# Merge-gate projections by Strassen's seven block products, with stored activation sums, in a hybrid attention block

## The chip, the core and the metric

The kernel runs on one core of a Trainium2 chip. The metric is the device time of one execution in microseconds, as the median of several runs. The engines are called by the names of the profile: PE (TensorE, the matrix engine; PEld is its weight load), DVE (VectorE), ACT (ScalarE), POOL (GpSimd) and SP (SyncE, which issues most DMAs here).

## The reference

One decoder layer over 512 tokens of width 1024, in float32:

```python
h = rms_norm(x, norm_g)                       # (512, 1024)
proj = h @ w_in                               # (1024, 6152)
fq, fk, fv, fz, mq, mk, mv, mz, ga, gb, fl = split_cols(proj, IN_SPLITS)
# 8 x 512 columns, then 1024 (ga), 1024 (gb), 8 (fl)
q, k = rms_norm(heads(fq), fox_q_g), rms_norm(heads(fk), fox_k_g)
log_f = log_sigmoid(fl + b_f)
y_fox = fox_attention(q, k, heads(fv), log_f) * silu(fz)      # 8 heads of 64
q, k = rope(rms_norm(heads(mq), moba_q_g)), rope(rms_norm(heads(mk), moba_k_g))
y_moba = moba_attention(q, k, heads(mv)) * silu(mz)           # 8 heads of 64
merged = (sigmoid(ga + b_gate[0]) * (y_fox @ w_fox)
          + sigmoid(gb + b_gate[1]) * (y_moba @ w_moba))
out = x + merged @ w_out
```

The two merge gates, `ga` and `gb`, are products of the normalised activations (512 x 1024) with 1024 columns of weights each. They are what the change is about. With two key blocks and a top-k of three, MoBA keeps every earlier block, so the kernel computes it as causal attention.

## The kernel before

Every matrix product is made of three matmuls on operands that are split in a high part and a remainder (`wh`/`wl` for weights, `Gh`/`Gl` for activations, `pth`/`ptl` for attention weights): high x high, high x remainder, remainder x high.

**Activations.** `load_g` reads the transposed x in 8 tiles of 128 x 512 (128 features, 512 tokens), multiplies them by `norm_g` and splits them into `Gh` (ACT) and `Gl` (DVE). They aren't divided by the root mean square. `x_stats` finds the factor `r` of each token later, from the untransposed x, and `x_bc` makes `rbc`, `r` spread over all partitions, by four transposes into the bank `p_rbc` and a copy on ACT. Each result is multiplied by `r` or `rbc` when it leaves PSUM: z units by DVE (`V.tensor_tensor(out=z, in0=p, in1=rbc, ...)`, tiles `zs_…`), then a sigmoid on ACT and a product on POOL; values by `evac_v`; queries and keys by the head norm `norm_qk`, whose small power `ff` and product `qn` are on POOL. POOL also applies the rotation in `do_rope`.

**Weights.** They come in chunks of 256 columns, in two halves of 4 x 128 rows each (512 KB). `load_half` issues a load on SP's queue into one of two buffers `wr` and calls `split`: ACT writes `wh` (128x1024), and the remainder `wl` is written in two pieces of 128x512, one on DVE and one on POOL (for `fka` and `fza` both on DVE). `load_branch` does the same for `w_fox` and `w_moba`, 512 columns at a time, and `load_out` for `w_out`. The chunks are named by projection and half: `fqa` is the first half of fq, `mzb` the second of mz; `ga0` to `ga3` and `gb0` to `gb3` are the gates, `wf0`, `wf1`, `wm0`, `wm1`, `wo0` to `wo3` the rest.

**Gates.** A gate unit makes 128 columns for all 512 tokens (`tr_mm`, lines 287 to 295): 8 row tiles x 3 matmuls of 512 columns, into a bank `pj`. `unit_ga` multiplies by `rbc`, applies the sigmoid and multiplies by the FoX branch `FS` (made by `unit_f`); `unit_gb` keeps the sigmoid for `unit_m`, which adds both branches and splits the merged rows into `mgh`, `mgl` for the output projection (`first_o`, `unit_o`).

**Order.** Each engine works off its own queue in order. The order of the program below is written by hand; when the kernel is built, a scheduler's timeline may still move single instructions within it. The program starts with `fqa` and `fka` over all tokens at once (`first_qk`), then x_stats, the z gates, the first values, and the forget gates (`forget`: a chain of small 128x32 DVE instructions `fg`, a cumulative sum by matmuls into `p_c`, and a table `LR` by transposes into `p_LR`). Then there are four attention groups of four heads. Each has steps `Tr` (transposes into `p_qT`, `p_kT`, splits, and copies of `KH` between partitions by DMA), `Aa` (scores and softmax; `lg`), `Bb` (transposes of the weights, their split, value matmuls into `pv`, and the pair `ypair`), `Yp` (product with the z gate and its split). `inter` mixes these steps with projection units:

```python
seq(["fza", "fzb", "fva"])
forget()
inter(attn_group("f", "a", ...), filler(["fqb", "fkb", "fvb"]))
inter(attn_group("f", "b", ...), filler(["mqa", "mka", "mva"]))
moba_begin()
seq(["mza", "mzb"])
inter(attn_group("m", "a", ...), filler(["mqb", "mkb", "mvb"]))
inter(attn_group("m", "b", ...), filler(["wf0", "wf1", "ga0"]))
seq(["ga1", "ga2", "ga3", "gb0", "gb1", "wm0", "gb2", "gb3", "wm1"])
first_o()
seq(["wo1", "wo2", "wo3"])
```

`filler` issues the loads and splits of the next chunk after the first unit of the present one.

## Time and profile before

| | before |
|---|---|
| runs, us | 442.98 (median), 442.8, 444.35 |
| span of the profiled execution, us | 440.8 |
| that execution's own time | the page gives none beside the span; the runs lie 2.0 to 3.6 us above the span |
| busy: PE / DVE / ACT / POOL, us | 433.9 / 277.9 / 231.1 / 178.1 |
| matmuls | 2804 |
| data moved by DMA | 45.85 MB, 104 GB/s on average |
| granted clock of TensorE | 9 tenths or more in all slices |

The profile is one execution on the chip, in microseconds from the start of its span. An engine's busy time is what its own instructions take; register and semaphore instructions and the issuing of DMAs are not in it. A row of the timeline gives start, duration, engine, line, operation, output and inputs, shape, and in brackets how long the engine had been idle before it and what it waited for. Grouped rows give the count, the total, and the mean in nanoseconds; rows by tile give minimum, median and maximum in nanoseconds and the stretch in which they lie. The page's part 2 divides the span into 40 slices of 11.0 us with the busy share in tenths.

### The profile page before, as it was taken

The page shows a single profiled execution, that of the slowest core. Times are in us where ns is not written, and L with a number is a line of the kernel's source. Part 1 is how long each engine was busy: PE and PEld are TensorE (multiplying, and loading weights), DVE is VectorE, ACT ScalarE, POOL GpSimd, SP SyncE. Part 2 cuts the span into 40 slices and gives each one's busy share as a digit, 9 for nine tenths or more (in the row PEclk, how much of TensorE's full clock was granted, in tenths as well). Part 3 has the DMA queues.
Part 4 walks back from the last instruction along what each step waited for, and adds up shares of the span by engine and source line. Part 5 has one row for each costly group of instructions (what it writes and reads, how often), then busy time and mean ns, then how long its engine had stood idle before and what let it go on. Part 6 is the DMA issues. An engine that isn't in the chain of part 4 may idle for free.

```text
span 440.8 us, 7535 instructions
## 1 busy us (share of the span) xinstructions
PE 433.9 (98%) x2804; PEld 394.0 (89%) x2804; DVE 277.9 (63%) x606; ACT 231.1 (52%) x439; POOL 178.1 (40%) x159
## 2 busy tenths in 40 slices
PE   7999999999999999999999999999999999999996
PEld 6998899999999998889999888888888888889996
DVE  4649626999789896248977868786442482373311
ACT  5866237867766754357866677564333333331200
POOL 6059624327347472555575222052333333322400
PEclk9999999999999999999999999999999999999999
DMA  8942225312243022231220422122222223335511
GB/s 256 366 151 100 95 97 148 95 55 99 65 105 121 3 94 97 95 120 25 96 97 1 145 81 75 36 97 90 96 101 86 91 72 114 116 119 160 189 62 48
DMA packets 18933, 45.85 MB, mean 104 GB/s; under 512 B 2576, under 2 KB 6800, under 8 KB 18896
## 3 DMA queue, kind: packets, MB, share of 16 engines
q1 hardware_dynamic: 16160, 43.13, 30.5%
q10 hardware_dynamic: 2736, 2.23, 1.5%
q8 instruction: 22, 0.36, 0.3%
q14 instruction: 15, 0.12, 0.1%
HBM read 39.98 MB, written 2.10 MB: 95 GB/s over the span
## 4 chain that ended last, share of the span: by engine, by line
PE 93%; DMA 2%; DVE 2%; ACT 1%; issue 0%; SPq 0%; ACTq 0%
PE pga L295 3%; PE pgb L295 3%; PE pga L294 3%; PE pga L293 3%; PE pgb L294 3%; PE pgb L293 3%; PE po L608 3%; PE po L609 3%; PE po L610 3%; PE lg L428 2%; PE pv L458 2%; PE lg L429 2%; PE pv L457 2%; PE pf L508 2%; PE pm L510 2%; PE pf L510 2%
## 5 line engine op out<-in xcount | busy, mean ns | idle before, releaser
L433 ACT ACTIVATE p<-p,negm 128x128 f32<-128x128 f32 (+1 forms) x64 | 35.7, 560 | 27.1 <-DVE negm L431 26.7
L222 POOL TENSOR_TENSOR ff<-ss,mh 128x8 f32<-128x8 f32 x16 | 27.9, 1750 | 34.3 <-DVE ss L220 31.1
L431 DVE CUSTOM_DVE_ANT_0 p<-lg,mask 128x128 f32<-128x128 f32 (+1 forms) x64 | 30.7, 485 | 11.3 <-PE lg L429 10.6
L436 DVE TENSOR_SCALAR p<-p,rinv 128x128 f32<-128x128 f32 (+1 forms) x64 | 31.3, 497 | 1.2
L102 POOL TENSOR_TENSOR wl_wo<-wr_o,wh_wo 128x512 fp32r<-128x512 f32 x8 | 14.1, 1758 | 32.8 <-ACT wh_wo L99 32.8
L608 PE MATMUL po<-wh_wo,mgh 128*128 128x256 f32 x96 | 27.1, 282 | 0.0
L610 PE MATMUL po<-wh_wo,mgl 128*128 128x256 f32 x96 | 26.9, 281 | 0.0
L609 PE MATMUL po<-wl_wo,mgh 128*128 128x256 f32 x96 | 26.9, 281 | 0.0
L102 POOL TENSOR_TENSOR wl_gb<-wr_gb,wh_gb 128x512 fp32r<-128x512 f32 x8 | 14.3, 1787 | 31.0 <-ACT wh_gb L99 31.0
L293 PE MATMUL pga<-Gh,wh_ga 128*128 128x512 f32 x64 | 25.6, 400 | 0.0
L102 POOL TENSOR_TENSOR wl_ga<-wr_ga,wh_ga 128x512 fp32r<-128x512 f32 x8 | 12.1, 1516 | 33.2 <-ACT wh_ga L99 28.6
L294 PE MATMUL pga<-Gl,wh_ga 128*128 128x512 f32 x64 | 25.5, 399 | 0.0
L295 PE MATMUL pga<-Gh,wl_ga 128*128 128x512 f32 x64 | 25.4, 397 | 0.0
L295 PE MATMUL pgb<-Gh,wl_gb 128*128 128x512 f32 x64 | 25.3, 395 | 0.0
L293 PE MATMUL pgb<-Gh,wh_gb 128*128 128x512 f32 x64 | 25.2, 393 | 0.0
L294 PE MATMUL pgb<-Gl,wh_gb 128*128 128x512 f32 x64 | 25.2, 393 | 0.0
L428 PE MATMUL lg<-KH,QS 128*128 128x128 f32 (+1 forms) x64 | 20.7, 329 | 0.5 <-DMA KH<-KH 0.4
L618 DVE TENSOR_TENSOR ot<-po,xr 128x256 f32<-128x256 f32 x16 | 6.6, 424 | 22.2 <-PE po L610 17.4
L99 ACT ACTIVATE wh_wo<-wr_o 128x1024 fp32r<-128x1024 f32 x8 | 8.5, 1061 | 21.6 <-DMA out_dram<-ot 8.0
L609 PEld LDWEIGHTS po<-wl_wo,mgh 128*128 128x128 f32 x96 | 18.1, 189 | 0.0
L610 PEld LDWEIGHTS po<-wh_wo,mgl 128*128 128x128 f32 x96 | 18.1, 189 | 0.0
L608 PEld LDWEIGHTS po<-wh_wo,mgh 128*128 128x128 f32 x96 | 18.1, 189 | 0.0
(389 smaller groups left out, 1628.5 us busy)
## 6 DMA issues: line engine op xcount, KB each, us to landing
wr_ga<-in_w_in_dram SPq DMA_DIRECT2D x8, 512.0 KB
wr_gb<-in_w_in_dram SPq DMA_DIRECT2D x8, 512.0 KB
wr_o<-in_w_out_dram SPq DMA_DIRECT2D x8, 512.0 KB
xt<-in_xT_dram SPq DMA_DIRECT2D x8, 256.0 KB
x<-in_x_dram SPq DMA_DIRECT2D x8, 256.0 KB
KH<-KH SPq DMA_DIRECT2D x16, 128.0 KB
wr_wf<-in_w_fox_dram SPq DMA_DIRECT2D x4, 512.0 KB
wr_wm<-in_w_moba_dram SPq DMA_DIRECT2D x4, 512.0 KB
```

The lines of the kernel that those rows point to most:

```text
L102: eng.tensor_tensor(out=lo[:, q, 0:n], in0=src[:, q], in1=hi[:, q, 0:n].bitcast(F32), op=OP.subtract)
L222: G.tensor_tensor(out=f2, in0=ss.rearrange("p t h -> p (t h)"), in1=mh, op=OP.pow)
L293: T.matmul(p, hi[:, k, cc], Gh[:, kk, :], start=(kk == 0), stop=False)
L294: T.matmul(p, hi[:, k, cc], Gl[:, kk, :], start=False, stop=False)
L295: T.matmul(p, lo[:, k, cc], Gh[:, kk, :], start=False, stop=(kk == KT - 1))
L428: T.matmul(lg[:, :n], qs[:, qt], kh[:, :n], start=True, stop=False)
L431: V.tensor_tensor_reduce(pt, lg[:, :n], mask[:, 512 - n:512], -0.125, 3.0e38, op0=OP.add, op1=OP.min, accum_out=mkn[:, hh, i:i + 1])
L433: A.activation(pt, pt, AF.Exp, bias=mkn[:, hh, i:i + 1], scale=-1.0, accum_out=rs[:, hh, i:i + 1])
L436: V.tensor_scalar(pt, pt, ri[:, hh, i:i + 1], None, op0=OP.mult)
L608: T.matmul(p[:, :CW], gh[:, st], hi[:, k, :CW], start=(kk == 0), stop=False)
L609: T.matmul(p[:, :CW], gh[:, st], lo[:, k, :CW], start=False, stop=False)
L610: T.matmul(p[:, :CW], gl[:, st], hi[:, k, :CW], start=False, stop=(kk == KT - 1))
```

## The change

The two gates are no longer 16 units of 24 matmuls with 512 columns. The normalised activations and the weights of a group of 512 gate columns (256 of one half and 256 of the other) are each seen as 2 x 2 blocks: two halves of the tokens by two halves of the features, and two halves of the features by two sets of 256 columns. Seven products of blocks give the result, in Winograd's form of Strassen's scheme, where the plain way has eight. A product is 2 x 4 x 3 matmuls with 256 columns. There are four groups, `GA0`, `GA1` (ga) and `GB0`, `GB1` (gb).

- Products take the block A11, A22 or A12 of the activations, or one of four sums S1 to S4. `normalise` makes normalised `Gh` and `Gl` first; the four sums over four row tiles, split in high part and remainder, are made once by `make_sums` and written to DRAM, 32 stores of 128 KB on SP's queue. `load_sums` reads them back before the gates, 8 loads of 512 KB on POOL's queue.
- The unnormalised activations stay as `Z` for `fqa`, `fka`, `fza`, `fzb`; every later projection uses the normalised ones, and its factor `r` or `rbc` falls away. The z gates of the MoBA branch take their sigmoid straight from PSUM, and their product is on DVE in place of POOL.
- The weight sums are made in place in the load buffers by `prep`: three differences on DVE and one on POOL per group, then `split` with the remainder whole (128x1024) on one engine.
- Seven products share three banks. `keep` copies a bank to SBUF on ACT, `add` joins it with another bank on DVE, and `finish` applies the sigmoid.
- Buffers: `wr` 4 for 2, tag `y` 15 for 17, `pt` 6 for 7. Pools are opened and closed by stage (start, attention, gates, end), and a tile waits for those that held its place before. `pump` issues loads up to four buffers ahead and splits up to three ahead.
- Order: `mzb` moves from before the first MoBA group into the second, `wf` and `wm` are cut in chunks of 256 columns.

The core of the diff:

```diff
+WR = 4
...
+        for k in range(KT):                                        # normalise()
+            V.scalar_tensor_tensor(XT[k], XT[k], col(C_NG + k), rbc, op0=OP.mult, op1=OP.mult)
+            A.activation(Gh[:, k, :], XT[k], AF.Copy)
+            V.tensor_tensor(out=Gl[:, k, :], in0=XT[k], in1=Gh[:, k, :].bitcast(F32), op=OP.subtract)
...
+    def make_sums():
...
+        for k in range(4):
+            a, b = XT[k], XT[k + 4]
+            f = [sf() for _ in range(4)]
+            G.tensor_tensor(out=f[2], in0=a[:, 0:HT], in1=a[:, HT:S], op=OP.subtract)
+            G.tensor_tensor(out=f[0], in0=a[:, HT:S], in1=b[:, HT:S], op=OP.add)
+            G.tensor_tensor(out=f[1], in0=f[0], in1=a[:, 0:HT], op=OP.subtract)
+            G.tensor_tensor(out=f[3], in0=b[:, 0:HT], in1=f[1], op=OP.subtract)
+            for s in (2, 1, 0, 3):
+                hi, lo = [stage["pool"].tile([P, HT], F32R, name=f"sp{hl}", tag=f"sp{hl}", bufs=3) for hl in "hl"]
+                A.activation(hi, f[s], AF.Copy)
+                V.tensor_tensor(out=lo, in0=f[s], in1=hi.bitcast(F32), op=OP.subtract)
+                nc.sync.dma_start(out=S_dram[0][s][:, k], in_=hi.bitcast(F32))
+                nc.sync.dma_start(out=S_dram[1][s][:, k], in_=lo.bitcast(F32))
+
+    def load_sums():
+        for s in (2, 1, 0, 3):
+            SB[s] = [stage["pool"].tile([P, 4, HT], F32R, name=f"S{s}{hl}") for hl in "hl"]
+            for hl in range(2):
+                nc.gpsimd.dma_start(out=SB[s][hl].bitcast(F32), in_=S_dram[hl][s])
...
-        A.activation(v[:, t, :, 0:HD], pv, AF.Copy, scale=r[:, t:t + 1])
-        V.scalar_tensor_tensor(v[:, t, :, HD:P], pv, r[:, t:t + 1], v[:, t, :, 0:HD].bitcast(F32),
-                               op0=OP.mult, op1=OP.subtract)
+        A.activation(v[:, t, :, 0:HD], pv, AF.Copy)
+        V.tensor_tensor(out=v[:, t, :, HD:P], in0=pv, in1=v[:, t, :, 0:HD].bitcast(F32), op=OP.subtract)
...
-            V.tensor_tensor(out=z, in0=p, in1=rbc, op=OP.mult)
-            A.activation(s, z, AF.Sigmoid)
-            G.tensor_tensor(out=z, in0=z, in1=s, op=OP.mult)
+            if name[0] == "f":
+                V.tensor_tensor(out=z, in0=p, in1=rbc, op=OP.mult)
+                A.activation(s, z, AF.Sigmoid)
+                G.tensor_tensor(out=z, in0=z, in1=s, op=OP.mult)
+            else:
+                A.activation(s, p, AF.Sigmoid)
+                V.tensor_tensor(out=z, in0=p, in1=s, op=OP.mult)
...
+    PRODUCTS = (("A11", 1), ("S3", 3), ("S2", 1), ("A22", 3), ("S1", 1), ("S4", 1), ("A12", 2))
...
+                if n == 1:                                         # prep(n) of a group
+                    sub(R["11"], R["12"], R["11"], V)
+                    sub(R["12"], R["22"], R["12"], G)
+                elif n == 2:
+                    sub(R["12"], R["22"], R["11"], V)
+                elif n == 3:
+                    sub(R["12"], R["21"], R["12"], V)
+                key, eng = (("11", V), ("12", V), ("12", V), ("12", V), ("11", V), ("22", G), ("21", G))[n]
+                B[n] = split(R[key], CW, f"{name}{n}", eng)
...
+            if n in (0, 1, 6):                                     # product(n)
+                st[b] = pst(("pj", "tp", "tp")[b - 1], (2, 3, 3)[b - 1], f"pb{b}_{name}")
+            p = st[b]
+            hi, lo = B[n]
+            for c in range(2):
+                o = p[:, c * HT:(c + 1) * HT]
+                cc = slice(c * P, (c + 1) * P)
+                for k in range(4):
+                    lh, ll = left(what, k)
+                    T.matmul(o, hi[:, k, cc], lh, ...)
+                    T.matmul(o, hi[:, k, cc], ll, ...)
+                    T.matmul(o, lo[:, k, cc], lh, ...)
...
+    order = ["fqa", "fka", "fza", "fzb", "fva", "fqb", "fkb", "fvb", "mqa", "mka", "mva", "mza",
+             "mqb", "mkb", "mvb", "mzb", "wf0", "wf1", "wf2", "wf3", "GA0", "GA1", "GB0", "wm0", "wm2",
+             "GB1", "wm1", "wm3", "wo0", "wo1", "wo2", "wo3"]
...
+    normalise()
+    pump(0)
+    seq(["fza", "fzb"])
+    make_sums()
+    seq(["fva"])
+    forget()
+    enter("attention")
...
-    seq(["mza", "mzb"])
+    seq(["mza"])
     inter(attn_group("m", "a", col(C_MQ), col(C_MK)), filler(["mqb", "mkb", "mvb"]))
-    inter(attn_group("m", "b", col(C_MQ), col(C_MK)), filler(["wf0", "wf1", "ga0"]))
...
+    inter(attn_group("m", "b", col(C_MQ), col(C_MK)), filler(["mzb", "wf0", "wf1", "wf2"]))
+    enter("gates")
+    load_sums()
+    seq(["wf3", "GA0", "GA1", "GB0", "wm0", "wm2", "GB1"])
+    enter("end")
+    seq(["wm1", "wm3"])
...
```

More of the change, by code (lines that the diff above doesn't have):

```diff
@@ L159, in fox_moba_kernel @@
     mh = con.tile([P, 8], F32, name="mh")
-    rbc = con.tile([P, S], F32, name="rbc")
     def x_stats():
@@ L173, in x_stats, with normalise @@
         G.tensor_tensor(out=r, in0=mm, in1=mh[:, :NT], op=OP.pow)
-    def x_bc():
+    rbc = con.tile([P, S], F32, name="rbc")
+    def normalise():
         p = pst("lg", 2, "p_rbc")
@@ L530, in go, with unit_m @@
+    def unit_m(i, c):
         def go():
             j = 2 * i + c
[L532 to L543 removed]
@@ L574, in go @@
+            V.tensor_tensor(out=u, in0=u, in1=FS[i][:, c, :], op=OP.add)
+            if i % 2:
+                mh_, ml_ = (stage["pool"].tile([P, S], F32R, name=f"mg{hl}{j}", tag="mg", bufs=8) for hl in "hl")
+            else:
+                mh_, ml_ = (t2("y", 15, f"mg{hl}{j}", dt=F32R) for hl in "hl")
             A.activation(mh_, u, AF.Copy)
@@ L577, in unit_m @@
         return go
-    def load_out(n):
-        for hf in range(2):
-            raw = sb.tile([P, 4, CW], F32, name=f"wr_o{n}{hf}", tag="wr", bufs=2)
-            nc.sync.dma_start(out=raw, in_=w_out[n, :, 4 * hf:4 * hf + 4, :])
-            chunks.setdefault(f"wo{n}", []).append(split(raw, CW, f"wo{n}{hf}"))
     def first_o():
@@ L658, in filler, with go @@
         for nm in names:
[L659 to L668 removed]
+            for n, u in enumerate(units(nm)):
+                def go(i=first_prep[nm] + (n if nm[0] == "G" else 0), u=u):
+                    pump(i)
+                    u()
+                res.append(go)
         return res
@@ L684, in seq @@
             u()
-    loaded.update(("fqa", "fka"))
+    enter("start")
     nc.scalar.dma_start(out=wfl, in_=w_fl)
@@ L699, in fox_moba_kernel @@
         evac_qk(b2[t], "fka", t)
-    ensure("fza")
+    normalise()
[5 more added lines that the diff above has]
+    enter("attention")
     zero_kl()
-    x_bc()
-    seq(["fza", "fzb", "fva"])
-    forget()
     rope_tables()
```

329 lines of the change are left out of this document (190 added, 139 removed).

## The prediction

> **What bounds the kernel now.** I read the page's part 1 first, then the slices of part 2, then the chain of part 4.
>
> ```profile
> span 440.8 us, 7535 instructions
> PE 433.9 (98%) x2804; PEld 394.0 (89%) x2804; DVE 277.9 (63%) x606; ACT 231.1 (52%) x439; POOL 178.1 (40%) x159
> ...
> PE   7999999999999999999999999999999999999996
> ...
> DVE  4649626999789896248977868786442482373311
> ...
> POOL 6059624327347472555575222052333333322400
> PEclk9999999999999999999999999999999999999999
> ...
> PE 93%; DMA 2%; DVE 2%; ACT 1%; issue 0%; SPq 0%; ACTq 0%
> ```
>
> TensorE is busy in 38 of 40 slices at full clock and makes 93% of the chain. Only 440.8 - 433.9 = 6.9 us of it stand idle, in the first and last slices. So two things move the time and nothing else: fewer matmul microseconds, and new waits in TensorE's queue. A microsecond of either counts in full. DVE and POOL have room on average. Where the change adds work, slices 4 to 7 (33 to 77 us), DVE stands at 9, 6, 2, 6 tenths and POOL at 9, 6, 2, 4: 25 and 23 us of 44.
>
> **What Strassen takes away.** Busy time of a matmul overlaps its neighbour's, so I price by starts, from the timeline of TensorE: a gate stretch, an output stretch, and four transposes from the chain.
>
> ```profile
> 371.66 0.39 PE L293 MATMUL pgb<-Gh,wh_gb 128*128 128x512 f32 x1
> ...
> 380.69 0.40 PE L508 MATMUL pm<-yhm,wh_wm 128*128 128x512 f32 x1
> ...
> 397.19 0.28 PE L593 MATMUL po<-wh_wo,mgh 128*128 128x256 f32 x1
> ...
> 399.31 0.28 PE L593 MATMUL po<-wh_wo,mgh 128*128 128x256 f32 x1
> ...
> 115.73 0.44 PE p_qT L392 x4
> ```
>
> Between the first two rows lie 39 matmuls of 512 columns: 9.03 / 39 = 0.2315 us each. Between the next two lie 18 of 256 columns: 2.12 / 18 = 0.1178 us. Transposes of 128 columns take 0.11 us each, so 0.11 is near a floor, but 256 columns still stand above it.
> Before: 16 gate units x 24 = 384 matmuls x 0.2315 = 88.9 us. After: 4 groups x 7 products x 24 = 672 x 0.1178 = 79.2 us. Gain 9.7 us. Every other matmul stays; some are reordered.
>
> **What the new vector work costs at the start.** The gates' operand must now be a true sum of normalised activations, so x_stats is followed by `normalise` (8 multiplications and 8 subtractions of 128x512 on DVE, 8 copies on ACT) and `make_sums` (16 sums of 128x256 on POOL, 16 copies on ACT, 16 subtractions on DVE, 32 stores on SP's queue). All of it is put between the first two projections and the first attention group. ACT's part (8 x 0.6 and 16 x 0.4 us) is waited for by DVE only. Whether DVE and POOL can do this side by side is shown by these rows: two timeline rows, two stretches of min/median/max by tile, then a DVE instruction that reads PSUM.
>
> ```profile
> 81.99 3.01 POOL L102 TENSOR_TENSOR wl_fvb<-wr_fvb,wh_fvb 128x512 fp32r<-128x512 f32 x2 [3.51 <-PE lg L429]
> ...
> 82.37 3.18 DVE L102 TENSOR_TENSOR wl_fvb<-wr_fvb,wh_fvb 128x512 fp32r<-128x512 f32 x2
> ...
> L102 DVE TENSOR_TENSOR wl_ga<-wr_ga,wh_ga x8: 693/1457/1777, 249.8 to 304.2; 128x512 fp32r<-128x512 f32 x8
> ...
> L341 DVE SCALAR_TENSOR_TENSOR fg<-fg,fg x7: 182/194/1223, 39.8 to 43.0; 128x32 f32<-128x32 f32 x7
> ...
> 272.00 1.81 POOL L102 TENSOR_TENSOR wl_ga<-wr_ga,wh_ga 128x512 fp32r<-128x512 f32 x1 [7.01 <-ACT wh_ga L99]
> ...
> 273.28 0.69 DVE L454 TENSOR_TENSOR ptl<-p_a,pth 128x512 fp32r<-128x512 f32 x1
> ```
>
> A DVE subtraction of two SBUF tensors takes 0.69 us alone and up to 1.78 beside POOL; a 128x32 one, 0.19 alone, takes 1.22. In the first pair POOL runs, then DVE, POOL, DVE: 82.0 to 85.55 is the sum of all four, not the longer side. The DVE row at 273.28 has one operand in PSUM and keeps 0.69 though POOL runs until 273.8. So two-SBUF work on DVE and POOL's work take turns, and their times add: 25 + 23 us of now and some 26 us of new work (below) don't fit into 44, even with the parts that need no turn. The Trainium skill says the same ("SBUF — State Buffer", section "Who interferes with whom"): a DVE instruction with two SBUF inputs and a GpSimd instruction that reads SBUF exclude each other for a whole instruction. It speaks against this change, and the trace agrees with it: 0.69 against 1.78.
>
> Prices and places in the present order:
>
> ```profile
> L224 POOL TENSOR_TENSOR qn_fka<-qn_fka,ff 128x512 f32<-128x512 f32 x2 | 2.1, 1039 | 0.0
> ...
> L307 POOL TENSOR_TENSOR zs_fza<-zs_fza,sg 128x512 f32<-128x512 f32 x2 | 2.6, 1294 | 2.6 <-ACT sg L306 2.6
> ...
> L261 POOL TENSOR_TENSOR qn_mqa<-ra,rb 128x128 f32<-128x128 f32 x2 | 0.9, 461 | 0.2
> ...
> 47.65 0.68 DVE L305 TENSOR_TENSOR zs_fza<-pz_fza,rbc 128x512 f32<-128x512 f32 x1
> 48.25 0.68 DVE L102 TENSOR_TENSOR wl_fva<-wr_fva,wh_fva 128x512 fp32r<-128x512 f32 x1
> ...
> 31.60 0.44 PE p_rbc L178 x4
> ...
> 33.56 0.61 ACT L179 ACTIVATE rbc<-p_rbc 128x512 f32<-128x512 f32 x1
> ...
> 36.98 3.69 POOL L222 TENSOR_TENSOR ff<-ss,mh 128x8 f32<-128x8 f32 x2
> ...
> 43.00 0.39 PE L293 MATMUL pz_fzb<-Gh,wh_fzb 128*128 128x512 f32 x1
> ...
> 48.55 0.40 PE L293 MATMUL pz_fzb<-Gh,wh_fzb 128*128 128x512 f32 x1
> ...
> 57.30 0.36 PE L197 MATMUL pj_fva<-wh_fva,Gh 128*128 128x256 f32 x1
> ```
>
> DVE starts follow each other by 0.60 us. A POOL sum of 128x256 isn't in the trace; between 0.46 (128x128) and 1.29 (128x512) I take 0.70. A DVE subtraction of 128x256: between 0.19 and 0.60, I take 0.34.
> In the built order the transposes p_rbc stand 19 matmuls (4.4 us) later than now, at 36.0, so rbc is there at 37.0 and the multiplications begin. TensorE needs Gh and Gl only for fva, from 48.55 + 24 x 0.2315 = 54.1 on: 17.1 us later. That covers DVE's own work, but three other waits lie in it.
> (1) The second fzb unit needs the bank that the eviction zs of the second fza unit frees. On DVE there stand before and with it 8 multiplications, 6 subtractions, one weight subtraction, two evictions and a small one: 17 x 0.60 + 0.2 = 10.4 us, alone until 47.4, and TensorE needs it at 48.55. But POOL, done with the pows of fka at about 40 (now 36.98 + 3.69 = 40.7), has nine instructions ready in the same time (three qn, three sums, two weight subtractions, one zs): 3 x 1.04 + 3 x 0.70 + 3 x 1.29 = 9.1 us. Taking turns, all nine go first: about 56. That is 7.4 us late.
> (2) The forget gates' cumulative sum p_c and the second fva unit behind it wait for the fg chain and the next zs. Between lie 6.9 us on DVE (the last Gl, five spl, two weight subtractions, ten small ones, two zs) and 7.8 us on POOL (two zs, four sums, two weight subtractions): 56 + 14.7 - 0.6 (a PSUM eviction that takes no turn) = 70. TensorE now gets there at 57.30. Total delay 12.8 us.
> (3) Later waits (p_LR, the first heads' copies) are met by a TensorE that is already late. SP's queue holds weight loads for fvb and mqa and the first heads' KL and KH copies behind the 32 stores, and they too have those 12 us.
> Bounds: 0 if POOL's instructions find DVE's gaps, 12.8 if each turn is taken. The rows at 82 us show turns taken every time, but some of POOL's sums wait for DVE's spl and can't press; I take 10.5.
>
> **What else is added.** The last lines:
>
> ```profile
> L483 DVE TENSOR_TENSOR ypair<-pv,ysh 64x512 f32<-64x512 f32 x16 | 11.0, 686 | 3.4 <-ACT ysh L482 3.3
> L482 ACT ACTIVATE ysh<-pv 64x512 f32<-64x512 f32 x16 | 9.5, 593 | 7.0 <-PE pv L458 6.7
> L99 ACT ACTIVATE wh_gb<-wr_gb 128x1024 fp32r<-128x1024 f32 x8 | 8.5, 1060 | 8.9 <-PE pga L294 5.5 <-PE pgb L294 2.9 <-PE pm L509 0.5
> 192.85 4.51 DMA KH<-KH
> ```
>
> End of attention: the third product reuses the first one's bank, whose copy `keep` stands on ACT behind the last head's pair (ysh 0.59, two DVE steps of 0.69, a split of 0.6, then the copy 0.59: 3.2 us and four handovers). One product, 24 x 0.1178 = 2.8 us, covers it: 0.9 us late; bounds 0 and 3.2.
> In a group, products 2 to 4 each need a DVE difference, an ACT copy and a DVE remainder in series on the same buffer. No 128x1024 DVE instruction is in the trace: by 2 x 0.60 it is 1.2, so 1.2 + 1.06 + 1.2 = 3.5 us against 2.8 of TensorE: 3 x 0.7 = 2 us behind per group. Four weight buffers let the splits run ahead, so I take 2 us for all four groups; bounds 0 and 8.
> At nothing: the eight loads of sums (POOL's queue; POOL then waits for attention's buffers, with only the remainders of products 6 and 7 behind it, needed 106 x 0.1178 = 12 us later), mzb moved from before the MoBA group into it (its 48 x 0.2315 = 11.1 us no longer cover rope and the KH copy of 4.51 us; 59 matmuls of mqb, 7 us, do; uncovered it costs 4), smaller pools with deeper weight prefetch.
>
> Sum by span: 440.8 - 9.7 + 10.5 + 0.9 + 2 = 444.5. The page gives no separate time of that execution; the median of the runs, 442.98, is 2.2 above the span. So 446.7 us.
>
> **Rivals.** *The collisions don't reach TensorE* (faster): the start costs under 4.6 us, because POOL comes late or DVE gets several turns in a row. Then 442.98 - 9.7 + 0.9 + 2 = 436.2 and up, to 440.8. For it: DVE's own work would be done at 47.4, before 48.55, so POOL being slow by some microseconds is enough and it can be late, since its order puts a weight subtraction and four pows first. Against: nine ready instructions of POOL, and the row at 82.37. It decides at about a third of the turns taken.
> *A draw*: start 4.6 to 9.1 us, 440.8 to 445.2.
> *The sums come late as well* (slower still): the loads are issued by POOL, and no DMA of POOL's queue is in the trace. If each took the 4.51 us of the KH row and ran one after the other, loads 3 and 4, released by the last scores, would land 9 us later. TensorE then has two products (5.7), 14 transposes (1.5) and 24 value matmuls (2.6 or more) ahead of their product, 9.8 us: just covered. At twice that price they are 8 us late: 455. The Trainium skill has a rule for it ("SBUF — State Buffer", the "DVE blocks DMA" trap): descriptors written by GpSimd wait while DVE runs a two-port instruction, and a DMA of 0.6 us took 3.1. By its figure loads 3 and 4 take 6.2 us and fit as well; no run here shows it yet.
> *It doesn't do what it says*: if 256 columns cost half of 512 exactly, 77.8 and not 79.2; if they fell to the floor of 0.11, 74. Either is within 5 us of the forecast, with no case of its own.
>
> **How the numbers follow.** Forecast case (start 9 to 13 us, 445.2 to 450): 0.45; sums late or groups at their bound (450 to 458): 0.14; draw 0.16; no collision 0.25. Predicted 446.7. The range leaves out some of either tail: 437 to 456. About 0.5% (2.2 us) is what can be told from no change here: below 440.8 faster 0.25, to 445.2 same 0.16, above it slower 0.59.
>
> **What would show it.** Right: TensorE idle in slices 4 to 7, 6 us or more before the second fzb unit with DVE's zs named as releaser, then at p_c; DVE's Gl and XT rows at means well over 0.69; DVE and POOL at 9 tenths together from 38 to 85 us; TensorE's matmul sum about 10 us smaller from 260 us on. Wrong: fva beginning at 54 to 56 us, or matmuls of the groups starting more than 0.125 us apart, or TensorE idle in the group stretch by more than 5 us in all.

## The result and the profile after

The changed kernel takes 454.31 us (median of five runs, 453.12 to 457.7) against 442.98: a ratio of 1.0258, 95% interval 1.0223 to 1.0292, or 11.3 us more. The forecast was 3.7 us more. The sign is right and the time lies in the range, but the loss is three times the forecast. The profiled execution is the longest of the five (457.7; span 456.0, mean granted clock 0.985), the other four have spans of 451.4 to 452.8 at 0.992: sums by its trace explain 15 us, not 11.

First the page after: totals, the slices, and the chain by engine.

```profile
span 456.0 us, 8324 instructions
PE 433.2 (95%) x3092; PEld 406.6 (89%) x3092; DVE 319.1 (70%) x648; ACT 262.3 (58%) x497; POOL 190.2 (42%) x173
...
PE   7997689979999999999999999979999999999996
...
DVE  5579996748987999458997679853748287494411
...
POOL 5059677634243747335385211115060722523300
PEclk9999898989999999999999999989999999999999
...
PE 72%; DVE 13%; DMA 7%; issue 3%; ACT 3%; POOL 0%; SPq 0%; DVEq 0%; ACTq 0%
```

TensorE has lost full slices at three places: slices 4 to 6 (34 to 68 us), slice 9 and slice 27. The clock row, all nines before, has eights in slices 5, 7, 9 and 27. DVE now makes 13% of the chain (2% before). What TensorE waited for, with the total, the number of waits and the longest:

```profile
PE pz_fzb L374 <- DVE zs_fza L387: 6.3, 2, 3.2
PE lg L512 <- DMA KH<-KH: 3.4, 2, 2.9
PE pv L541 <- DVE ypair L567: 2.7, 1, 2.7
...
PE pb_GB L665 <- DVE wl_GB L112: 1.4, 2, 0.8
...
PE p_c L434 <- DVE fg L428: 1.1, 1, 1.1
PE pj_fva L275 <- DVE zs_fzb L387: 0.9, 1, 0.9
PE pb_GA L665 <- DVE wl_GA L112: 0.5, 1, 0.5
```

These come to 16.3 us; before, nothing but the two waits at the very start (1.5 and 1.2) and one of 0.4 stood in this view. What follows a wait is seen in windows of TensorE alone (stretch, length, busy time and instructions, granted clock, DMA share, GB/s):

```profile
31.20:54.40 23.20, 17.59 (x78) 1.00 0.17 58
54.40:57.60 3.20, 2.48 (x6) 0.52 0.57 168
57.60:68.20 10.60, 8.63 (x52) 0.98 0.47 146
68.20:71.80 3.60, 3.60 (x20) 0.53 0.85 248
71.80:95.00 23.20, 20.29 (x172) 1.00 0.69 202
95.00:98.60 3.60, 3.60 (x21) 0.57 0.48 153
98.60:300.20 201.60, 198.50 (x1419) 1.00 0.29 87
300.20:303.70 3.50, 3.38 (x13) 0.52 0.90 355
303.70:456.00 152.30, 146.72 (x1125) 1.00 0.33 107
```

Four windows of 3.2 to 3.6 us at about half clock stand right behind waits: that of the second fzb unit, the pair at `p_c` and the second fva unit, that of the first scores and that at the end of attention. The longest wait of all, the 3.20 us of the first fzb unit, has none behind it: the first window, in which it lies, stands at 1.00. Each spell costs half its length, about 1.7 us; over the span, 456.0 x (1 - 0.985) = 6.8 us. Waits and half clock together are 23.1 us. Less the 9.7 us that the gates save, that is 13.4 of the 15.2 us by which the span grew; the remaining 2 us lie in small gaps. By stage:

| | forecast, us | profiled execution, us |
|---|---|---|
| first z unit to first fqb matmul | +10.5 | +12.0: waits 3.2 + 3.1 + 1.1 + 0.9 = 8.3, half clock 3.4 |
| first scores of FoX | 0 | +4.6: wait 2.9, half clock 1.7 |
| rest of attention | 0 | -1.0 |
| end of attention | +0.9 | +4.4: wait 2.7, half clock 1.7 |
| gate products | +2 | +5: waits 1.9, the rest in restarts and small gaps |
| fewer matmul microseconds | -9.7 | -9.7 |

In the runs with clock 0.992 half as much is lost to the clock (452.6 x 0.008 = 3.6 us), so these add up to about 12.

The start on its engines, from the timelines of TensorE, DVE and POOL:

```profile
46.17 0.47 PE L374 MATMUL pz_fzb<-Zh,wh_fzb 128*128 128x512 f32 x1 [3.20 <-DVE zs_fza L387]
...
55.12 0.80 PE L374 MATMUL pz_fzb<-Zh,wh_fzb 128*128 128x512 f32 x1 [3.13 <-DVE zs_fza L387]
...
37.50 7.92 DVE L220 SCALAR_TENSOR_TENSOR xt<-xt,cs,rbc 128x512 f32<-128x512 f32 x8
45.34 0.68 DVE L387 TENSOR_TENSOR zs_fza<-pz_fza,rbc 128x512 f32<-128x512 f32 x1
46.53 4.43 DVE L222 TENSOR_TENSOR Gl<-xt,Gh 128x512 fp32r<-128x512 f32 x3
...
54.38 0.68 DVE L387 TENSOR_TENSOR zs_fza<-pz_fza,rbc 128x512 f32<-128x512 f32 x1
...
36.42 3.31 POOL L303 TENSOR_TENSOR ff<-ss,mh 128x8 f32<-128x8 f32 x2
39.71 1.43 POOL L305 TENSOR_TENSOR qn_fqa<-qn_fqa,ff 128x512 f32<-128x512 f32 x1
41.10 1.19 POOL L236 TENSOR_TENSOR sf<-xt 128x256 f32<-128x256 f32 x1
...
58.41 0.73 POOL L239 TENSOR_TENSOR sf<-xt,sf 128x256 f32<-128x256 f32 x1
```

DVE's eight multiplications take 0.99 us each instead of 0.60, because POOL's head norms lie in the same stretch. So the eviction of the first fza unit ends at 46.0, and already the first fzb unit waits for it. The eviction of the second fza unit ends at 55.1, and the second fzb unit waits for that one. POOL's sum of 128x256 takes 1.19 us beside DVE's multiplications and 0.73 at 58.41, where DVE's next subtraction waits for it instead.

### The profile page after: what moved, and what is told of

Its sections match the earlier page's. It is cut to its first block, busy times and chain, and to the rows that moved or that the text cites. A ratio compares the mean times of both kernels' runs of the same rounds, so it can differ in the third digit from the quotient of the medians.

```text
span 456.0 us, 8324 instructions
## 1 busy us (share of the span) xinstructions
PE 433.2 (95%) x3092; PEld 406.6 (89%) x3092; DVE 319.1 (70%) x648; ACT 262.3 (58%) x497; POOL 190.2 (42%) x173
## 4 chain that ended last, share of the span: by engine, by line
PE 72%; DVE 13%; DMA 7%; issue 3%; ACT 3%; POOL 0%; SPq 0%; DVEq 0%; ACTq 0%
PE po L762 2%; PE po L764 2%; PE po L763 2%; PE pv L541 2%; PE pv L542 2%; PE lg L512 2%; PE lg L513 2%; DMA KH<-KH 2%; PE pb_GB L665 2%; DMA s_dram<-spl 2%; PE pb_GA L662 2%; PE pb_GA L665 2%; PE pb_GA L664 2%; PE pb_GB L662 2%; PE pb_GB L664 2%
## 5 line engine op out<-in xcount | busy, mean ns | idle before, releaser
L116 POOL TENSOR_TENSOR wl_wo<-wr_wo,wh_wo 128x512 fp32r<-128x512 f32 x8 | 12.2, 1532 | 27.4 <-ACT wh_wo L110 27.4
L110 ACT ACTIVATE wh_wo<-wr_wo 128x1024 fp32r<-128x1024 f32 x8 | 8.5, 1059 | 21.0 <-PE po L764 7.7
L112 POOL TENSOR_TENSOR wl_GB<-wr_gb,wh_GB 128x1024 fp32r<-128x1024 f32 x4 | 10.1, 2540 | 24.9 <-ACT wh_GB L110 24.9
L110 ACT ACTIVATE wh_GB<-wr_gb 128x1024 fp32r<-128x1024 f32 x14 | 14.2, 1052 | 9.5 <-PE pb_GB L664 4.8
L110 ACT ACTIVATE wh_GA<-wr_ga 128x1024 fp32r<-128x1024 f32 x14 | 14.5, 1055 | 5.8 <-PE pb_GA L664 3.6
L112 POOL TENSOR_TENSOR wl_GA<-wr_ga,wh_GA 128x1024 fp32r<-128x1024 f32 x4 | 9.8, 2466 | 18.8 <-ACT wh_GA L110 18.8
L112 DVE TENSOR_TENSOR wl_GB<-wr_gb,wh_GB 128x1024 fp32r<-128x1024 f32 x10 | 12.5, 1265 | 6.7 <-ACT wh_GB L110 6.7
L512 PEld LDWEIGHTS lg<-KH,QS 128*128 128x128 f32 x64 | 12.1, 191 | 4.4 <-DMA KH<-KH 3.2
L567 DVE TENSOR_TENSOR ypair<-pv,ysh 64x512 f32<-64x512 f32 x16 | 11.0, 685 | 6.6 <-ACT ysh L566 6.5
L112 DVE TENSOR_TENSOR wl_GA<-wr_ga,wh_GA 128x1024 fp32r<-128x1024 f32 x10 | 12.1, 1223 | 4.6 <-ACT wh_GA L110 4.6
```

Of the source, the lines that this page charges most:

```text
L110: A.activation(hi[:, :, 0:n], src, AF.Copy)
L112: lo_on.tensor_tensor(out=lo[:, :, 0:n], in0=src, in1=hi[:, :, 0:n].bitcast(F32), op=OP.subtract)
L512: T.matmul(lg[:, :n], qs[:, qt], kh[:, :n], start=True, stop=False)
```

## The experiments

Ratios are to the kernel before on the same chip, with 95% intervals; single stretches come from each kernel's own trace. The theory was: DVE and POOL take turns at the start, and the stalls bring half clock. The rivals were: the store traffic on SP's queue, the amount of vector work whoever does it, and the matmuls' new form itself. One caution holds for all of them: single waits vary from trace to trace. In e7, e11 and e13 the instructions of the first 85 us stand in the order of the kernel after on TensorE, DVE, ACT and POOL, and no edit touches them. Yet their two fzb waits together come to 6.6, 3.7 and 5.9 us, for 6.3 there. A difference of 1 to 2 us between two traces is no measure of an edit.

**e1: the eight multiplications read the factor from PSUM.** The built order is the same.

```diff
-            V.scalar_tensor_tensor(XT[k], XT[k], col(C_NG + k), rbc, op0=OP.mult, op1=OP.mult)
+            V.scalar_tensor_tensor(XT[k], XT[k], col(C_NG + k), p, op0=OP.mult, op1=OP.mult)
```

> The eight multiplications of normalise read the spread factor from its PSUM bank and not from its SBUF copy. Each engine's order of instructions stays the same. Theory (two-SBUF instructions of DVE and POOL take turns): a DVE instruction with a PSUM operand takes no turn, so the eight take 8 x 0.68 = 5.4 us and not 7.9, TensorE's wait before the first fzb unit falls from 3.2 us to about 1, the waits behind it stay, and the time falls by 2 to 4 us, to 450 to 452. Rival (DVE simply has more work queued ahead of the evictions, whatever POOL does): the eight stay near 0.99 us each, the wait near 3 us, the time at 453 to 456.

454.29 us, 1.0228 [1.0183, 1.0273]. DVE's timeline, and TensorE's two waits:

```profile
36.77 5.35 DVE L220 SCALAR_TENSOR_TENSOR xt<-xt,cs,p_rbc 128x512 f32<-128x512 f32 x8
...
42.93 5.00 DVE L222 TENSOR_TENSOR Gl<-xt,Gh 128x512 fp32r<-128x512 f32 x3
...
42.86 0.47 PE L374 MATMUL pz_fzb<-Zh,wh_fzb 128*128 128x512 f32 x1 [1.18 <-DVE zs_fza L387]
52.60 0.50 PE L374 MATMUL pz_fzb<-Zh,wh_fzb 128*128 128x512 f32 x1 [3.95 <-DVE zs_fza L387]
```

With one operand in PSUM a multiplication takes 0.67 us beside the same POOL work: turn-taking is shown, and the first wait falls from 3.2 to 1.2. But POOL's work now meets the two-SBUF subtractions behind (three `Gl` in 5.00 us), and the second wait is 3.95 us, for 3.1, which is within what such waits vary. The time stays that of the kernel after, above the 450 to 452 expected. Freeing one step of a chain in which the whole chain is late did not win time here.

**e2: the stores away from the start.** The 32 stores of sums are left out; eight of 512 KB, of blocks of `Gh` and `Gl` in place of the sums, stand ahead of mza.

```diff
-                nc.sync.dma_start(out=S_dram[0][s][:, k], in_=hi.bitcast(F32))
-                nc.sync.dma_start(out=S_dram[1][s][:, k], in_=lo.bitcast(F32))
...
+    for s in range(4):
+        nc.sync.dma_start(out=S_dram[0][s], in_=Gh[:, 0:4, 0:HT].bitcast(F32))
+        nc.sync.dma_start(out=S_dram[1][s], in_=Gl[:, 0:4, 0:HT].bitcast(F32))
```

> The sums are made as in the changed kernel, but their 32 stores are left out; in their place eight stores of 512 KB of Gh and Gl blocks stand ahead of mza, so the gates get other data. Theory A (SP's queue and the DMA engines, full of stores, hold the first KH copies): the wait of 2.9 us at the first scores and the low clock after it go, the waits before fzb stay at 3 us each; time 449 to 451. Rival B (KH is late because its producers on ACT and DVE are late, stores or not): the wait at the first scores stays near 3 us, time 453 to 455.

456.72 us, 1.0295 [1.0253, 1.0336]. The first scores' wait fell from 2.9 to 1.0 us, but another of 1.4 came at 137 us, `p_c` waited 2.6, and the four waits of the start came to 8.7 us, for 8.3 in the kernel after. The time is above what either theory said. The stores alone don't make the loss.

**e3: no sums at all.** Sums, their splits and copies are left out; the stores take blocks of `Gh` and `Gl`.

```diff
-            G.tensor_tensor(out=f[2], in0=a[:, 0:HT], in1=a[:, HT:S], op=OP.subtract)
...
-                A.activation(hi, f[s], AF.Copy)
-                V.tensor_tensor(out=lo, in0=f[s], in1=hi.bitcast(F32), op=OP.subtract)
```

> POOL's 16 sums, ACT's 16 copies and DVE's 16 remainders are left out; the 32 stores stay and take blocks of Gh and Gl, so the gates get other data. Theory (turns): POOL and DVE each lose what presses the other, so the wait before the second fzb unit falls from 3.1 us to under 1.5, those at p_c and fva (1.1 and 0.9) go, and the multiplications come nearer to 0.6 us; time 446 to 449. Rival (normalise by itself, not the sums, makes the start late): both fzb waits stay near 3 us each and the time at 451 to 454.

449.29 us, 1.0115 [1.0091, 1.0138]. The first fzb unit still waits 3.4 us, and the eight multiplications still take 7.97: they are pressed by work of POOL that the kernel before has too. The other three waits of the start are gone. Of the 11.3 us the sums' vector work thus makes 0.0143 x 443 = 6.3, and what is left, `normalise` among it, about 5.

**e4: TensorE kept busy in the waits.** Twenty matmuls of zeros with 256 columns stand ahead of four waiting places.

```diff
+    def stir(n):
+        p = tp("stir")
+        for i in range(n):
+            T.matmul(p[:, :256], dum[:, :P], dum, start=True, stop=True)
```

> The changed kernel with 20 matmuls of 256 columns on zeros (2.4 us at full clock) put in front of each of the four long waits: before both fzb units that wait, before the first scores and before the last head's value product. No other instruction moves on TensorE. Theory C (an idle spell of some 3 us makes TensorE's clock fall to 0.5 for the next 3 to 4 us): granted clock 1.0 on the mean in place of 0.985 to 0.992, time 2 to 4 us less, 450 to 452. Rival D (the clock falls for another reason, or the waits are longer with the additional matmuls in the way): clock 0.985 to 0.992 and time 454 or more.

460.15 us, 1.0352 [1.0304, 1.0399]: as a time this is no answer, since the scheduler also moved DVE's work, and a wait of 4.8 us on `zs_fzb` is new. The windows do answer (busy of PE, PEld, DVE, ACT, POOL, then clock, DMA share, GB/s):

```profile
55.00:59.00 4.00, 3.17 (x14) 2.59 (x15) 4.00 (x7) 1.25 (x3) 2.48 (x2) 1.00 0.35 90
...
300.00:306.00 6.00, 5.48 (x46) 4.89 (x45) 3.67 (x7) 2.65 (x6) 1.07 (x2) 1.00 1.00 367
66.00:69.00 3.00, 0.00 (x0) 0.00 (x0) 3.00 (x4) 2.12 (x4) 3.00 (x3) 0.99 0.56 186
69.00:75.00 6.00, 4.82 (x22) 4.83 (x23) 6.00 (x12) 2.05 (x5) 5.86 (x6) 0.50 0.74 216
```

Where the zeros ran (55 and 300 us) the clock stayed at 1.00; behind the new idle stretch it fell to 0.50. So the low clock goes with idleness. The matmuls' new form does not bring it: in the kernel after, the window from 303.70 us on, which holds nearly all of the products, stands at 1.00.

**e5: the start made free.** `normalise` and the sums are left out: `Z` is the same as `Gh`, `Gl`, the eight stores stand as in e2.

```diff
-        for k in range(KT):
-            V.scalar_tensor_tensor(XT[k], XT[k], col(C_NG + k), rbc, op0=OP.mult, op1=OP.mult)
...
-    make_sums()
```

> The changed kernel without its new vector work at the start: no multiplications and no second split in normalise (the projections all read the unnormalised pair, so all results from the values on lack the factor r), no sums, and in place of the 32 stores eight stores of 512 KB of activation blocks ahead of mza. Gates, pools, weight prefetch and order stay. Theory (the loss is the start's vector work, the last head's wait, the products' weights and the low clock after long waits): what is left is 442.98 - 9.7 + 2.9 + 1.7 + 2.7 = 440.6; 438 to 442. Rival (the new pools, prefetch and order cost time of their own in attention): 445 or more.

442.45 us, 0.9997 [0.9980, 1.0015]. So the start's vector work and stores, with all that follows from them, cost 0.0261 x 443 = 11.6 us, as much as the whole loss. The first scores' wait is part of that: the longest wait for KH is 0.7 us here, for 2.9. What is left is the gates' gain of 9.7 eaten up by the end of attention, the products and the clock.

**e6: the sums on DVE.** `G.` becomes `V.` in the four sums of `make_sums`, the rest is unchanged.

> The 16 sums of 128x256 are made by DVE in place of POOL; nothing else in the program is edited, though the order built from it shifts. Theory (turns: what counts is the sum of DVE's two-SBUF work and POOL's work): 16 x 0.73 = 11.7 us on POOL become some 16 x 0.34 = 5.4 on DVE, so the pair has 6 us less to do; the waits at p_c and before the second fva unit shrink and the time falls by 2 to 5 us, to 449 to 452. Rival (DVE's queue alone is the bound, POOL only happens to be busy): DVE has 5.4 us more ahead of its evictions, the waits grow, 456 to 460.

453.09 us, 1.0219 [1.0187, 1.0252], between the theories: 1.7 us better than the kernel after, which the two intervals leave open. The first wait is 5.1, the second 0.8, fva's 2.3. With the sums gone from POOL the multiplications still take 7.97 us, since POOL's head norms are still there. Giving the sums to the other engine gains little; how the loss divides between turn-taking and the plain amount of DVE's work, this run doesn't say.

**e7: another bank for the last head's values.**

```diff
-                pv = pst("pv", 1, "pv")
+                pv = pst("lg", 2, "pv2") if br == "m" and half == "b" and h == 3 else pst("pv", 1, "pv")
```

> The last MoBA head's value product gets a bank of tag lg in place of the one bank pv, so that it needn't wait until the head before it is copied out. Theory: the wait of 2.7 us at 297 us shrinks to about 1 (DVE's splits of the last head end 1 us earlier than the pair), the clock stays at 1.0 behind it; 2 to 3.5 us less, 451 to 452. Rival (the splits of the last head are as late as the pair): the wait keeps its length under another name, 454 or more.

453.49 us, 1.0239 [1.0195, 1.0283]. The one wait of 2.7 us became two, and the clock there stayed at 1.0:

```profile
PE pv L542 <- DVE ptl L538: 0.8, 2, 0.5
```

So the bank of `pv` made the wait. The time misses the 451 to 452 expected and the gain is within the interval; e5 beside e10 shows it.

**e8: a wait put into the kernel before.** Between wo1 and wo2 TensorE is made to wait for two small powers on POOL.

```diff
+            if n == 2 and t < 2:
+                T.matmul(p[:, :8], ident, GP[0], start=True, stop=True)
...
+                for _ in range(2):
+                    G.tensor_tensor(out=g, in0=g, in1=mh, op=OP.pow)
```

> The kernel before, with one artificial wait: between the output chunks wo1 and wo2, TensorE waits for a small DVE instruction and two powers on POOL in series, some 4 us. Theory C (an idle spell of 3 to 4 us makes TensorE's clock fall to 0.5 for the next 3 to 4 us): the time grows by the wait and by a further 1.5 to 2 us, and the records show the clock at 0.5 right behind it; 448.5 to 449.5. Rival D (no link between idle time and clock): the wait alone, 447, clock 1.0.

451.6 us, 1.0201 [1.0177, 1.0226], or 9.0 us. POOL's own splits came between the powers, so the wait was longer than planned (the timeline, then the window after it):

```profile
421.15 0.60 PE L605 MATMUL po<-gp,ident 128*128 128x8 f32 x2 [6.31 <-POOL gp L618]
...
421.20:426.80 5.60, 5.60 (x26) 5.60 (x27) 0.00 (x0) 0.00 (x0) 0.00 (x0) 0.50 0.01 3
```

6.3 us of idleness and 5.6 us at half clock behind it (2.8 lost) are 9.1, beside the measured 9.0. This kernel has none of the change: the price of this wait is its length and the half clock after it.

**e10: e5 and e7 together.**

> The run with the free start (no normalising, no sums, other data for the gates) and the last head's own bank: what the seven products are worth when nothing else stands in their way. Theory: 442.5 of the free start less the wait of 2.7 us, of which 1.2 come back under the splits' name, and less 1.7 to 3.4 us of low clock: 438 to 440. Rival (the last head's wait costs nothing, since something else is late by as much): 442.

439.78 us, 0.9911 [0.9892, 0.9930], with a clock of 1.000. Beside e5 (on another chip, by ratios) the bank is worth 0.86% or 3.8 us: 1.9 of the wait of 2.7 (0.8 comes back at the splits) and the clock behind it. With a start that costs nothing the change would win 3.9 us of the gates' 9.7.

**e11, e13: the first scores' copy on another queue.** The copies `KH<-KH` go from SP's queue to ACT's (e11) or POOL's (e13). The theory was that they stand behind the stores in SP's queue.

```diff
-                    nc.sync.dma_start(out=kh[ot, :].bitcast(F32), in_=kh[me, :].bitcast(F32))
+                    nc.scalar.dma_start(out=kh[ot, :].bitcast(F32), in_=kh[me, :].bitcast(F32))   # e13: nc.gpsimd
```

> The changed kernel with the 16 KH copies between partitions issued by ACT, right behind the instruction that makes KH, and not in SP's queue behind weight loads and stores. Theory (the first scores wait for SP's queue): KH lands 2 to 3 us earlier, the wait of 2.9 us at the first scores falls under 1 and the low clock behind it goes; 2 to 4 us less, 450 to 452. Rival (the copy itself is slow because the DMA engines are full, or the first scores then wait for another operand): the wait stays over 2 us under this or another name, 453 to 456.

456.72 us, 1.0288 [1.0263, 1.0312]: the forecast of 450 to 452 fell. TensorE still waits 2.7 us, and now ACT is held for it. The chain of waits of the kernel after and then of e11, start and length, and last what SP's queue waited for in the kernel after:

```profile
83.39 5.16 DMA wr_mqa<-in_w_in_dram
...
88.62 5.22 DMA KH<-KH
...
84.18 5.22 DMA wr_mqa<-in_w_in_dram
...
89.47 4.95 DMA KH<-KH
...
SPq L489 <- DMA wr_mqa<-in_w_in_dram: 0.6, 1, 0.6
```

On either queue the copy is issued when the half load `wr_mqa` has landed. In the built program each DMA of these two queues waits for the one eight places ahead of it, and from the issue of that half load at 83.39 the copy is the eighth (four stores, the second half load, a KL and a Q copy, KH). The two queues differ in what this hold adds. In the kernel after ACT has made KH at 83.6, but SP's queue works off the stores, the half load and two copies first and comes to KH only at 88.0, so the hold adds 0.6 us. In e11 ACT has made KH at 84.4 and the hold alone keeps it until 89.4. So the queue did stand in the way, and leaving it wins nothing while the load eight places ahead lands no sooner. Without the stores the wait was 1.0 us (e2).

> The changed kernel with the 16 KH copies issued by POOL on its own queue. In SP's queue, and in ACT's in the run before, a copy has to wait until the eighth DMA before it has landed (for the first KH copy that is the first half of mqa's weights, 5.2 us from issue to landing); on POOL's queue there are no others at that time. Theory (that hold): the first KH copy is issued 1 to 3 us sooner after ACT has made KH, and the wait of 2.7 to 2.9 us at the first scores falls under 1, or goes over to another operand that is still in SP's queue; the time falls by 1 to 4 us, to 451 to 454. Rival (a copy takes 5 us because the DMA engines are full): it still takes 5 us from issue to landing and the wait stays.

456.18 us, 1.0269 [1.0222, 1.0315]. The first copy on POOL's queue, the lengths of the first two KH copies from issue to landing, and a Q copy on SP's queue:

```profile
87.03 0.75 POOL L489 DMA_DIRECT2D KH<-KH  x1
...
DMA to landing us min/median/max: 6.0/6.3/6.6
...
88.84 6.57 DMA Q<-QS
```

The copy was issued 1.6 us earlier, but it took 6.6 us in place of 5.2 and landed at 93.65, no sooner than the 93.84 of the kernel after. TensorE no longer waits for it only because it comes to the first scores later, at 93.7 instead of 91.0. It then waits 1.5 us for the Q copy, which took three times the 2.2 us of the one Q copy whose landing the trace of the kernel after holds. So the rival stands here: with the hold gone the copies are slow, while the DMA engines are 0.88 busy (87.0 to 93.65 us). Queue order, hold and load follow each other; how much each would give by itself, these runs don't say.

**e9, e12, e14, e15: the whole computation, with the work rearranged.** In e9 the multiplications read PSUM, fva uses `Z` with `r` as before, six of the eight copies and subtractions to `Gh`, `Gl` are tied behind the eviction of the second fza unit, the sums are made on DVE within the first attention group, and e7's bank is taken. e12 adds the copy KH on ACT's queue and the weight remainders of fva and fqb on DVE. e14 and e15 make each product's weight differences, copy and remainder in two halves (KH on POOL, on ACT).

```diff
 e9
+            if k < 2:
+                A.activation(Gh[:, k, :], XT[k], AF.Copy)
+            else:
+                A.activation(Gh[:, k, :], XT[k], AF.Copy, scale=PR[1])   # 1.0, from the second fza unit
...
+        def both(u=fl[k + 1], m=make_sums(k)):
+            u()
+            m()
 e12
-            eng = G if q.start and name[:3] not in ("fka", "fza") else V
+            eng = G if q.start and name[:3] not in ("fka", "fza", "fva", "fqb") else V
 e14, e15
+            for q in (slice(0, 2), slice(2, 4)):
+                A.activation(hi[:, q, 0:n], src[:, q], AF.Copy)
+                lo_on.tensor_tensor(out=lo[:, q, 0:n], in0=src[:, q], in1=hi[:, q, 0:n].bitcast(F32), op=OP.subtract)
```

> The whole computation, with the start arranged by what the first eight runs showed: the multiplications read the factor from PSUM; fva reads the unnormalised pair and gets its factor r on eviction as before, so that Gh and Gl are needed only for fqb; six of the eight splits wait for the eviction of the second fza unit; the sums are made by DVE, two to a tile, and their splits and stores stand beside the units of the first attention group; the last head has its own bank. Theory (turns, and evictions queued behind splits): both fzb waits and the one before the second fva unit go, 1 to 3 us of waits appear in the first attention group, the time is 441 to 445. Rival (the vector work is too much for the first 130 us wherever it stands): 447 to 452.

> The whole computation: the rearranged start, with the KH copies issued by ACT and the remainders of the fva and fqb weights all on DVE (POOL took 1.3 to 2.1 us for each). Theory (POOL's long instructions hold the small DVE steps ahead of p_c; SP's queue holds KH): the waits of 2.3 us at p_c and of 3.7 us at 131 us both fall under 1 and take their low clock with them; 443 to 446. Rival (DVE is full and SP's queue not the cause): 449 to 452.

> The second rearrangement, with the KH copies issued by POOL, and with each difference, copy and remainder of the products' weights cut in two pieces of 128x512, so that a product can begin on the first. Theory: the three waits of 0.5 to 0.8 us on the fourth products go (a chain of 0.6 + 0.6 + 0.6 and then one piece more, in place of 1.2 + 1.06 + 1.2), and the wait for KH at 127 us of 1.7 too; 440 to 442.5, below the kernel before. Rival (more instructions on DVE and ACT cost as much as the chain gains): 444 to 446.

> As the run before, with the KH copies issued by ACT as in the second rearrangement, so that only the cut in halves differs from it. Theory: 2 to 2.5 us less than that one, 442 to 443. Rival: no change, 444 to 446.

| | us | ratio |
|---|---|---|
| e9 | 450.86 | 1.0173 [1.0149, 1.0197] |
| e12 | 444.95 | 1.0008 [0.9987, 1.0028] |
| e14 | 445.48 | 1.0033 [1.0007, 1.0060] |
| e15 | 443.11 | 0.9972 [0.9952, 0.9991] |

e9 came out in its rival's range, e12 in its theory's, e14 in its rival's and e15 just above its theory's. In e9 both fzb waits are at most 0.4 us, but `p_c` waits 2.3 and a copy KH at 131 us 3.7. e12 removes these (a KH wait of 1.7 is left). e15 is 0.3% below the kernel before (443.79 on that chip, 22 runs), less than the 0.5% that the prediction takes as the least that can be told from no change, and 2.8% below the change, by ratios. Its longest waits behind the first projection:

```profile
PE pb_GB L681 <- ACT e_GB L691: 2.5, 2, 1.6
...
PE pj_fva L285 <- DVE v_fva L324: 1.4, 1, 1.4
PE lg L530 <- DMA KH<-KH: 1.4, 1, 1.4
```

(This profiled execution is the shortest of its twelve, which reach from 440.25 to 443.75.) The three waits on weight remainders are gone, and a wait on the copy of a bank has come in their place. Between e12 and e15, which differ in the halves alone, lie 0.36%, and their intervals overlap: whether the halves gain anything is not shown.

## Why the prediction was right in sign and short in size

**The gates' gain** (9.7 us) held. Matmuls of the groups start 0.119 us apart:

```profile
318.96 0.28 PE L662 MATMUL pb_GA<-S3h,wh_GA 128*128 128x256 f32 x1
...
320.98 0.28 PE L665 MATMUL pb_GA<-S3h,wl_GA 128*128 128x256 f32 x1
```

Between these rows lie 17 matmuls: 2.02 / 17. The 672 come to 79.8 us by that, for the 79.2 of the prediction. A start without cost (e10) gives 3.9 us of the 9.7 back as time.

**The start** (10.5 forecast, 12.0 in the profile): the mechanism held, and the size about, but not the split. (The 11.6 us of e5 are no second measure of it, since they hold the first scores' wait as well.) The step put a single long wait of 7.4 us ahead of the second fzb unit and took DVE to be alone until 47.4; in fact POOL pressed the multiplications too, and two fzb units waited 3.2 and 3.1 us. The first of the two was missed, and so the sign "6 us or more before the second fzb unit" didn't come. The end of the chain was right: the eviction put at about 56 ended at 55.1. The waits are 8.3 us, less than forecast, and the clock fills the rest. e1 shows that turn-taking is real (0.67 us for 0.99); e3 shows that the sums' vector work is about 6 of the 11 us, and that `normalise` beside POOL's old work still makes the first fzb unit wait 3.4 us. The rival *The collisions don't reach TensorE* fell with the first wait. Windows of the same stretch, of the kernel before and then of the kernel after (busy of PE, PEld, DVE, ACT and POOL, clock, DMA share, GB/s):

```profile
36.30:91.00 54.70, 54.70 (x386) 51.08 (x384) 37.23 (x86) 29.02 (x52) 29.40 (x21) 1.00 0.38 115
...
36.30:91.00 54.70, 46.37 (x288) 41.42 (x286) 46.93 (x78) 27.59 (x51) 41.41 (x40) 0.94 0.48 147
```

DVE rises by 9.7 us, POOL by 12, and TensorE has 8.3 us less: together 88 us of DVE and POOL in a stretch of 55, where part of what is counted is the pressing itself.

**The clock** is the step that failed, and the largest of four terms that were missed or too small. Each wait was priced at its length, at the full clock that the page of before shows in all its slices. That page couldn't show another price: its TensorE waits only 0.4 us after the first microseconds. 6.8 us of the profiled execution, 3.6 of the others, are lost that way. The span grew by 15.2 us for 3.7 forecast, and the difference adds up from the table: half clock 6.8 and the wait for the first KH copies 2.9, both put at nothing, the last head's wait 1.8 and the products 3 above their terms, less 2.2 by which the waits of the start stay under 10.5 and 1.0 in the rest of attention, 11.3 us together. With the 3.6 us of the other executions it is 8.1, beside the 7.6 by which the medians miss the forecast.

The Trainium skill ("TensorE: Matmul & The Clock Gate", "Part 1: The HAM clock gate") says that the clock halves after an idle window of about 3.4 us, a free-running one, and comes back after as long a busy one. The traces agree with the price, windows of 3.2 to 3.6 us at about 0.5; on the length they differ, since waits of 2.7 to 3.1 us, and two of 1.1 and 0.9 in a row, stand ahead of such spells too, while the one of 3.20 us has none. It was not weighed in the prediction.

**At nothing: the first copies KH** (4.6 us). The prediction said that SP's queue holds them behind the stores but that they "too have those 12 us". They had not: TensorE came to the first scores at 91.0, and the copy was issued at 88.62 and took 5.2 us. What made it late is shown only in part. The queue's order kept it until 88.0 and the hold until 88.6, and e13 shows that an earlier issue alone did not land it earlier. The prediction looked at the queue's order, and not at what its places wait for or how long a copy takes among that many transfers.

**End of attention** (0.9 forecast, 4.4): the bank was the wrong one. Not the product's bank with `keep` behind it but the single bank `pv` made the last head wait for the pair of the head before (2.7 us, gone in e7), because the order has no projection unit left between these two heads.

**Products** (2 forecast): the waits on the fourth product's remainder, 0.5 + 1.4 = 1.9 us, are as forecast and at the place given. Some 3 us more in small gaps were not in the sum.

**Sums from DRAM**: the eight loads on POOL's queue landed in 4.0 to 7.8 us, beside the 4.51 and 6.2 us of the prediction, and TensorE never waited for them. The rival *The sums come late as well* fell. The time is close to its 455, but by other causes.

## What to carry to other kernels

Where TensorE is busy all the time, price a new wait at its length and the half-clock spell that may follow it, 1.7 us or more: the four waits of about 3 us of the kernel after come to 12 us, and half clock adds 6.8 in the profiled execution and 3.6 in the others. Work that is "free" on engines with room on average must fit into the stretch before the first reader, counted with its neighbours on the other vector engine; otherwise move it to where TensorE has other work (with such moves, the other bank and smaller steps, e15 is some 12 us below the change and level with the kernel before). After a change that adds DMAs, follow the first transfers behind them back to what they wait for.

## What the runs showed of the hardware

- Half clock behind a wait is not certain. Waits of 3.4 us and more (e3 3.4, e7 3.7, e9 3.7, e13 3.8, e1 3.95, e4 4.8, e6 5.1, e8 6.3) always had a spell at 0.50 behind them. Below that the length doesn't decide: none followed 3.2 us (kernel after), 2.9 (e7) and 2.7 at the end of attention (e1, e6), while one followed the same 2.7 in the kernel after and in e5, 1.7 in e12, and two waits of 0.8 and 0.5 in a row in e15. A spell lasted about 3.4 us or, in e4, e5, e7 and e11, about 6.8. In e8 the clock fell during the wait itself (0.66 on the mean of it) and stayed at 0.50 for 5.9 us behind it.
- The trace of e13 has the landing of all sixteen 128 KB copies KH: 2.2 to 6.6 us, median 3.3. The first two, at 87 to 95 us, took 6.6 and 6.0, with the DMA engines 0.88 busy from 87.0 to 93.65 us; a copy `Q<-QS` in that stretch took 6.57. The trace of the kernel after has only two of the sixteen, 2.2 and 5.2 us.
